# Channel sums as rounded halves times rounded ones, and the keys' partner rows by four small transfers

## The chip, the cores and the metric

The kernel runs on one core of one Trainium2 chip. The metric is the device time of one execution in microseconds, the median of several runs. The core has a matrix engine (TensorE, PE in the rows), a vector engine (VectorE, DVE), a scalar engine (ScalarE, ACT), a general one (GpSimd, POOL) and a queue engine (SyncE, SP). Each engine works through its own list of instructions in the order of that list, and waits on semaphores for the others. Transfers are issued from the lists of SP, ACT and POOL.

## The reference, cut to what matters

Two layers work on 520 tokens (512 of a prompt, 8 of a decode step) with 1024 channels. Each layer takes a root-mean-square norm over the channels, multiplies by one wide input matrix, runs a 31-tap convolution branch and a sliding-window attention branch, and joins the two.

```python
def rms_norm(x, g):
    xf = x.astype(jnp.float32)
    y = xf * lax.rsqrt(jnp.mean(xf * xf, axis=-1, keepdims=True) + EPS)
...
def layer_norm(x, g, b):
    mu = jnp.mean(xf, axis=-1, keepdims=True)
    var = jnp.mean(jnp.square(xf - mu), axis=-1, keepdims=True)
    y = (xf - mu) * lax.rsqrt(var + EPS)
...
    h = rms_norm(x, norm_g)
    z = jnp.einsum('ntd,dc->ntc', h, w_in)
    u = glu[..., :CONV_WIDTH] * jax.nn.sigmoid(glu[..., CONV_WIDTH:])
    c = lax.conv_general_dilated(full, conv_w[:, None, :], ...) + conv_b
    c = jax.nn.silu(layer_norm(c, ln_g, ln_b)) * jax.nn.silu(gate_a)
    y_a = jnp.einsum('ntc,cd->ntd', c, w_conv_out)
    k = partial_rope(k.reshape(n, t, N_KV_HEADS, HEAD_DIM), pos)
    o, new_k, new_v = attend(q, k, v, sinks)
    y_b = jnp.einsum('nte,ed->ntd', o * jax.nn.silu(gate_b), w_attn_out)
    y = jax.nn.sigmoid(mg_a) * y_a + jax.nn.sigmoid(mg_b) * y_b
    return x + jnp.einsum('ntd,de->nte', y, w_out), new_conv, new_k, new_v
```

So three means over the 1024 channels are taken per layer (one of the root-mean-square norm, two of the layer norm), and the final norm takes one more. partial_rope rotates the first 16 of a head's 64 dimensions: dimension d below 8 is paired with d + 8.

## The kernel before

**Layout.** Channels lie on the 128 partitions and tokens along the free axis: a tile `g` is 128 x 520 in fp32, and eight of them hold a 1024-channel activation. All `g` tiles come from one ring of 42 buffers (`gp`, L52 and L69), which the tile framework hands out in program order: a tile can be written only when the tile 42 requests earlier has been read for the last time.

**Products.** A `Unit` (L101 to L145) computes 128 output channels for all tokens. Its weights arrive by SP into `raw` (2 buffers), are rounded on ACT into `whi` (L126, a CAST to fp32r) and subtracted on DVE into the rest `wlo` (L127). `step` (L130) issues three fp32r matmuls of 128x260 for each of eight channel blocks and each half of the tokens: 48 matmuls into one PSUM tile `mm`, of which there are two (L56). A unit can start only when the unit two before it has been copied out of PSUM. The two halves hi and lo of an activation come from `split` (L95), a CAST on ACT and a subtraction on DVE.

**Sums over channels.** `Sum` (L147) adds eight tiles on DVE into `ssum` (L165). `total` (L167) then sums over the partitions with a matmul by a 128x128 matrix of ones, in plain fp32, one for each half of the tokens. `totals` (L175) is called three times per layer: for the first norm (L290), for the layer norm's mean (L609) and for its variance (L615). The final norm calls `total` itself (L695). `rstd` (L178) makes 1/sqrt of a sum: Ln and Exp on ACT (L183, L186) and four operations on DVE (L184 to L189), and `normed` (L268) multiplies the layer's input by it (L271).

**The keys.** After the K unit (L339) its result is copied to `kn` on ACT (L343). A fp32 matmul by a permutation matrix `swap`, once for each half of the tokens (L352), puts each rotated dimension's partner in its row; DVE multiplies that by the sines (L353) and adds (L354). Rows 16 to 63 of a head have a sine of 0.

**The layer norm's place.** Attention scores of 32 blocks run first, interleaved with 16 units for the gates; the convolution (L599, on DVE) fills DVE beside them. Then come the 8 units of the gate GA (L622): each is copied out of PSUM by ACT (L624), gated by a sigmoid (L630) and a product (L631). The sums of the layer norm, the subtraction of the mean (L613) and the squares (L614, by L197) run among these units. Eight units YB (L644), eight YA (L650) and eight of the output product (L675) follow.

**The order.** The order on each engine is set by the tile framework's scheduler, which works from a modelled timeline; `tc.issue_after` and `cur_priority` give it hints. The list of each engine is then fixed. At the start x, the parameters and a table load are issued on ACT (L225, L202, L193), and the first weights and the rest of x on SP.

Of the kernel before, what the change touches and what calls it, by code (L numbers as in the profile page):

```python
# [10 lines left out]
F32R = mybir.dt.float32r  # L11
AF = mybir.ActivationFunctionType
ALU = mybir.AluOpType
# [6 lines left out]
HALF = TOK // 2  # L20
# [3 lines left out]
HD = 64  # L24
# [12 lines left out]
P_G, P_CW, P_CB, P_LG, P_LB, P_SK, P_SS = 0, 8, 256, 264, 272, 280, 296  # L37
N_P = 297

C_ID, C_SW, C_MASK, C_FG = 0, 128, 256, 512  # L40
N_C = 520


@with_exitstack
def hybrid_step(ctx, tc, x_in, w_in, par, const, rope, conv_st, kc_in, vc_in,
                y_out, ncp, nkp, nvp, ncs, nks, nvs):
    nc = tc.nc
    V, A, PE, G = nc.vector, nc.scalar, nc.tensor, nc.gpsimd

    cst = ctx.enter_context(tc.tile_pool(name="cst", bufs=1))  # L50
# [14 lines left out]
    def name(p):  # L65
        uid[0] += 1
        return f"{p}{uid[0]}"

    def g(dt=F32):  # L69
        return gp.tile([128, TOK], dt, tag="g", name=name("g"))  # L70
# [4 lines left out]
    def two(t):  # L75
        return t.rearrange("p (a b) -> p a b", a=2)

    def sbank():
        return psS.tile([128, 512], F32, tag="S", name=name("S"))
# [6 lines left out]

    con = cst.tile([128, N_C], F32, name="con")
    ident = con[:, C_ID:C_ID + 128]
    swap = con[:, C_SW:C_SW + 128]
    ones = cst.tile([128, 128], F32, name="ones")  # L90
    V.memset(ones, 1.0)
    eps = cst.tile([128, 1], F32, name="eps")
    V.memset(eps, EPS)

# [52 lines left out]
    class Sum:  # L147
# [18 lines left out]

        def total(self, hf):  # L167
            ps = sbank()[:, :HALF]
            last = self.left.get(hf)
            PE.matmul(ps, ones, two(self.acc)[:, hf, :], start=True, stop=last is None)  # L170
            if last is not None:
                PE.matmul(ps, ones, last, start=False, stop=True)  # L172
            return ps

        def totals(self):  # L175
            return [self.total(0), self.total(1)]

    def rstd(sums, halves=(0, 1)):  # L178
        y0, v, a = tmp("y0", 1), tmp("v", 1), tmp("a", 1)
# [78 lines left out]
    for l in range(L):  # L258
        last = l + 1 == L
# [19 lines left out]
        for i in range(KT):  # L279
# [39 lines left out]
            if i % 2 == 1:  # L319
# [7 lines left out]
                for i in pair:  # L327
                    V.tensor_tensor(pr4[:, i - i0], st[i0 // 2][:, i - i0],
                                    wv[:, i - i0].unsqueeze(1).broadcast_to([128, NS, TAPS]),
                                    op=ALU.mult)  # L330
# [6 lines left out]


        kps = Unit(l, W_K, hh, hl).both()  # L339
        kn, kcos, ksin, krot = g(), g(), g(), g()  # L340
        nc.gpsimd.dma_start(kcos, rope[2])
        nc.gpsimd.dma_start(ksin, rope[3])
        A.copy(two(kn), kps)  # L343
        V.tensor_tensor(krot, kn, kcos, op=ALU.mult)
        vps = Unit(l, W_V, hh, hl).both()
        vt = g()
        A.copy(two(vt), vps)
        nc.gpsimd.dma_start(nvp[l], vt[:, T - 128:T])
        for hf in range(2):
            c = slice(hf * HALF, (hf + 1) * HALF)  # L350
            kss = sbank()
            PE.matmul(kss[:, :HALF], swap, kn[:, c], start=True, stop=True)  # L352
            V.tensor_tensor(ksin[:, c], kss[:, :HALF], ksin[:, c], op=ALU.mult)  # L353
        V.tensor_tensor(krot, krot, ksin, op=ALU.add)  # L354
        nc.gpsimd.dma_start(nkp[l], krot[:, T - 128:T])
        KH, KL = [], []
        for kv in range(2):
# [9 lines left out]
        for j in range(2):  # L367
            t = g()
# [37 lines left out]
        for j in range(2):  # L406
            t = g()
# [38 lines left out]
        for t in range(8):  # L446
            ps = Unit(l, W_GB + t, hh, hl).both()
# [173 lines left out]
        for i in range(KT):  # L621
            ps = Unit(l, W_GA + i, hh, hl).both()  # L622
# [12 lines left out]
        for i in range(KT):  # L635
            c = cs[i]
# [7 lines left out]
            ps = Unit(l, W_YB + i, oh, ol).both()  # L644
# [4 lines left out]
        for i in range(KT):  # L649
            ps = Unit(l, W_YA + i, ch, cl).both()  # L650
# [17 lines left out]
        if not last:  # L668
# [5 lines left out]
            for i in range(KT):  # L674
                ps = Unit(l, W_OUT + i, yh, yl).both()  # L675
# [68 lines left out]
def _constants():  # L744
    f = np.float32
    con = np.zeros((128, N_C), f)
    r = np.arange(128)
    con[r, C_ID + r] = 1
    d = r % HD
    partner = np.where(d < 8, r + 8, np.where(d < 16, r - 8, r))  # L750
    con[r, C_SW + partner] = 1
    j = np.arange(256)[None, :]
    q = r[:, None]
    ok = np.where(j < 128, j > q, j - 128 <= q)
    con[:, C_MASK:C_MASK + 256] = np.where(ok, 0, NEG)
    pos = np.concatenate([np.arange(T), np.full(NS, PAST)]).astype(f)
    inv = (f(500000.0) ** (-np.arange(0, 16, 2, dtype=f) / f(16))).astype(f)
    ang = pos[None, :] * inv[:, None]
    cos, sin = np.cos(ang).astype(f), np.sin(ang).astype(f)
    rope = np.zeros((4, 128, TOK), f)  # L760
    rope[0] = cos[r % 8]
    rope[1] = sin[r % 8]
    rope[2] = np.where((d < 16)[:, None], cos[d % 8], 1)
    rope[3] = np.where((d < 8)[:, None], -sin[d % 8], np.where((d < 16)[:, None], sin[d % 8], 0))
    return con, rope.astype(f)
# [63 lines left out]
```

## Time and profile before

| what | us |
|---|---|
| median of 3 runs | 1073.75 (1073.62 to 1073.75) |
| the profiled execution | 1073.94 |
| its span in the trace | 1071.8 |
| PE busy | 1058.2 (99%) |
| DVE busy | 855.4 (80%) |
| ACT busy | 515.0 (48%) |
| POOL busy | 77.5 (7%) |

The span is the time from the first to the last instruction of the trace; the profiled execution's own time is 2.1 us longer. PE's matmuls are pipelined: an instruction's own duration (284 ns for a 128x260 one) overlaps the next one's, so what one costs is read from the distance between the starts of two, or from a stretch of the chain that ended last. A plain fp32 matmul shows as two records, an fp32r one as one. Layer 1 repeats layer 0 some 525 us later.

### The profile page before, as it was taken

Reading aid. Unit: us, or ns where it says so; the run is one execution under the profiler, and the core shown is the slowest. Engines: PE = TensorE matmul, PEld = TensorE weight load, DVE = VectorE, ACT = ScalarE, POOL = GpSimd, SP = SyncE. Lnnn points to the kernel's source line nnn. Section 1 sums busy time; section 2 is a strip of 40 time slices with the busy share of each in tenths; the row PEclk is TensorE's granted clock in tenths of the full one; section 3 lists DMA queues with packets and bytes.
Section 4 is the critical chain, followed back from the end, with each engine's and each line's share of the span. In section 5 each row is a group of like instructions: output and inputs, shape, how many; then the busy total and the mean of one; then the engine's idle time right before and its main releaser. Section 6 shows DMA issues by size and latency. Waiting matters only on the chain.

```text
span 1071.8 us, 21521 instructions
## 1 busy us (share of the span) xinstructions
PE 1058.2 (99%) x8738; PEld 1036.0 (97%) x8738; DVE 855.4 (80%) x1570; ACT 515.0 (48%) x951; POOL 77.5 (7%) x185
## 2 busy tenths in 40 slices
PE   8999999999999999999999999999999999999996
PEld 8999999999999999999999999999999999999995
DVE  6999999999999586455569999999999976944545
ACT  7621433366666784223453234334675686822321
POOL 1111211000000000000101113100000000000000
PEclk9999999999999999999999999999999999999998
DMA  7334574332322225233334337623232213242212
GB/s 250 108 119 136 167 245 134 116 100 80 115 79 65 70 69 189 89 99 119 138 92 138 119 126 239 204 100 118 80 119 67 92 41 99 91 171 95 99 59 80
DMA packets 44371, 126.41 MB, mean 118 GB/s; under 512 B 6208, under 2 KB 8976, under 8 KB 44272
## 3 DMA queue, kind: packets, MB, share of 16 engines
q1 hardware_dynamic: 37728, 110.23, 31.0%
q0 software_dynamic: 5104, 13.33, 3.9%
q10 hardware_dynamic: 1440, 1.48, 0.4%
q8 instruction: 68, 1.11, 0.4%
q14 instruction: 31, 0.25, 0.1%
HBM read 107.66 MB, written 17.36 MB: 117 GB/s over the span
## 4 chain that ended last, share of the span: by engine, by line
PE 98%; DVE 1%; DMA 0%; ACT 0%; issue 0%; ACTq 0%; DVEq 0%
PE mm L134 87%; PE S L510 3%; PE pv L545 3%; PE PT L536 2%; PE T L134 1%; DVE g L700 1%; PE V L134 1%; PE S L170 1%; DMA par<-par 0%; PE S L468 0%; PE pvs L490 0%; PE S L352 0%; DVE g L689 0%; PE S L172 0%; PE S L396 0%
## 5 line engine op out<-in xcount | busy, mean ns | idle before, releaser
L134 PE MATMUL mm<-g,whi 128*128 128x260 f32 x4160 | 772.8, 284 | 1.9 <-ACT g L212 1.8
L134 PEld LDWEIGHTS mm<-g,whi 128*128 128x128 f32 x4160 | 647.6, 189 | 8.5 <-issue 5.7
L134 PE MATMUL mm<-g,wlo 128*128 128x260 f32 x2080 | 589.1, 283 | 0.0
L134 PEld LDWEIGHTS mm<-g,wlo 128*128 128x128 f32 x2080 | 392.4, 189 | 0.9 <-issue 0.8
L599 DVE SCALAR_TENSOR_TENSOR acc<-u,par,acc 128x512 f32<-128x512 f32 x464 | 328.3, 743 | 0.2
L126 ACT CAST whi<-raw 128x1024 fp32r<-128x1024 f32 (+2 forms) x166 | 172.6, 1040 | 207.7 <-PE mm L134 167.8
L127 DVE TENSOR_TENSOR wlo<-raw,whi 128x1024 fp32r<-128x1024 f32 (+2 forms) x166 | 200.3, 1208 | 53.5 <-ACT whi L126 53.3
L134 PE MATMUL mm<-o,whi 128*128 128x260 f32 x992 | 179.3, 282 | 1.0 <-DVE g L689 1.0
L134 PEld LDWEIGHTS mm<-o,whi 128*128 128x128 f32 x992 | 153.1, 188 | 1.5 <-issue 0.8
L134 PE MATMUL mm<-o,wlo 128*128 128x260 f32 x496 | 139.5, 282 | 0.0
L134 PEld LDWEIGHTS mm<-o,wlo 128*128 128x128 f32 x496 | 93.2, 188 | 0.0
L522 ACT ACTIVATE p<-p,sm 128x257 f32<-128x257 f32 (+1 forms) x128 | 60.8, 478 | 10.7 <-DVE sm L516 10.6
L538 ACT COPY pts<-PT 128x256 f32<-128x256 f32 (+1 forms) x64 | 33.8, 528 | 60.6 <-PE PT L536 60.3
L516 DVE CUSTOM_DVE_ANT_0 p<-S,con,nsk 128x256 f32<-128x256 f32 (+1 forms) x128 | 52.6, 446 | 10.8 <-PE PT L536 8.9
L514 POOL COPY p<-nsk 128x2 f32<-128x2 f32 x64 | 21.7, 345 | 351.5 <-PE PT L536 276.4
L651 DVE TENSOR_TENSOR g<-mm,g 128x520 f32<-128x520 f32 x16 | 11.2, 699 | 42.9 <-PE mm L134 42.9
L510 PE MATMUL S<-g,g 128*128 128x256 f32 x256 | 42.4, 285 | 0.0
L449 ACT ACTIVATE g<-mm 128x520 f32<-128x520 f32 x16 | 9.7, 605 | 56.8 <-PE mm L134 56.8
L645 DVE TENSOR_TENSOR g<-mm,g 128x520 f32<-128x520 f32 x16 | 11.1, 695 | 32.1 <-PE mm L134 32.1
L510 PEld LDWEIGHTS S<-g,g 128*128 128x128 f32 x256 | 35.2, 188 | 0.8 <-DVE sm L516 0.8
L536 PE MATMUL PT<-con,p 128*128 128x128 f32 x224 | 35.6, 276 | 0.0
L526 ACT ACTIVATE p<-p,sm 128x128 f32<-128x128 f32 (+1 forms) x64 | 29.9, 480 | 8.9 <-DVE sm L525 8.9
(169 smaller groups left out, 821.0 us busy)
## 6 DMA issues: line engine op xcount, KB each, us to landing
raw<-w SPq DMA_DIRECT2D x162, 512.0 KB, 3.4
qscr<-g SPq DMA_DIRECT2D x32, 256.0 KB, 4.4
g<-qscr SPq DMA_DIRECT2D x32, 256.0 KB, 3.7
g<-x SPq DMA_DIRECT2D x15, 260.0 KB, 4.8
g<-rope POOLq DMA_DIRECT2D x8, 260.0 KB, 4.6
xres<-g POOLq DMA_DIRECT2D x8, 260.0 KB, 2.3
g<-xres SPq DMA_DIRECT2D x8, 260.0 KB, 5.1
g<-conv_state POOLq DMA_DIRECT2D x8, 248.0 KB, 3.2
```

Of the source, the lines that this page charges most:

```text
L126: mark[2] = A.copy(self.hi[:, ks, :], self.raw[:, ks, :])
L127: mark[0] = V.tensor_tensor(self.lo[:, ks, :], self.raw[:, ks, :], self.hi[:, ks, :].bitcast(F32), op=ALU.subtract)
L134: mark[1] = PE.matmul(self.acc[hf], a[:, k, :], b[k][:, c], start=(k == 0 and j == 0), stop=(k == KT - 1 and j == 2))
L510: PE.matmul(S3[:, kv, :], qs[t, kv][:, b * 128:b * 128 + 128], K[kv][:, k0:k0 + 256], start=(j == 0), stop=(j == 1))
L514: G.tensor_copy(p[:, :, nk:nk + 1], nsk[:, 2 * t:2 * t + 2].unsqueeze(2))
L516: V.tensor_tensor_reduce(out=p[:, kv, :nk], in0=S3[:, kv, :nk], in1=con[:, C_MASK + 256 - nk:C_MASK + 256], op0=ALU.add, op1=ALU.min, scal ...
L522: exp_ins[0] = A.activation(p[:, kv, :nk + 1], p[:, kv, :nk + 1], AF.Exp, bias=nm[:, kv:kv + 1], scale=-1.0, accum_out=dn[:, kv:kv + 1])
L526: A.mul(p[:, 0, :nk], p[:, 0, :nk], dn[:, 0:1])
L536: PE.transpose(PT[:, kv, kb, :], p[:, kv, kb * 128:kb * 128 + 128], ident)
L538: A.copy(pts[t][:, :, j0:j0 + nb, :], PT[:, :, :nb, :])
L545: PE.matmul(pv[kv * 64:kv * 64 + 64, j * 128:(j + nb) * 128], vb[:, j * 128 + kv * 64:j * 128 + kv * 64 + 64], pts[t][:, kv, 2 * j:2 * j + ...
L599: V.scalar_tensor_tensor(dst, us[i][:, k:k + T], cw(i, k), acc[i], op0=ALU.mult, op1=ALU.add)
```

## The change

`totals` no longer multiplies the fp32 sum by fp32 ones. It splits the sum with `split` (a CAST on ACT into a `g` tile, a subtraction on DVE into another), and multiplies both by `ones_r`, the ones rounded to fp32r: two fp32r matmuls per half in place of one fp32 matmul. `ones_r` is made by ACT at the start of the program. The final norm's `total` stays fp32. For the keys, a tile `ks` is set to zero by POOL, four transfers of 8 rows each on POOL's queue copy the partner rows out of `kn`, and DVE multiplies the whole tile by the sines once. The permutation matrix leaves the constants.

```diff
--- before.py
+++ after.py
@@ -37,8 +37,8 @@
 P_G, P_CW, P_CB, P_LG, P_LB, P_SK, P_SS = 0, 8, 256, 264, 272, 280, 296
 N_P = 297
 
-C_ID, C_SW, C_MASK, C_FG = 0, 128, 256, 512
-N_C = 520
+C_ID, C_MASK, C_FG = 0, 128, 384
+N_C = 392
 
 
 @with_exitstack
@@ -86,9 +86,10 @@
 
     con = cst.tile([128, N_C], F32, name="con")
     ident = con[:, C_ID:C_ID + 128]
-    swap = con[:, C_SW:C_SW + 128]
     ones = cst.tile([128, 128], F32, name="ones")
     V.memset(ones, 1.0)
+    ones_r = cst.tile([128, 128], F32R, name="onesr")
+    A.copy(ones_r, ones)
     eps = cst.tile([128, 1], F32, name="eps")
     V.memset(eps, EPS)
 
@@ -166,14 +167,17 @@
 
         def total(self, hf):
             ps = sbank()[:, :HALF]
-            last = self.left.get(hf)
-            PE.matmul(ps, ones, two(self.acc)[:, hf, :], start=True, stop=last is None)
-            if last is not None:
-                PE.matmul(ps, ones, last, start=False, stop=True)
+            last = self.left[hf]
+            PE.matmul(ps, ones, two(self.acc)[:, hf, :], start=True, stop=False)
+            PE.matmul(ps, ones, last, start=False, stop=True)
             return ps
 
         def totals(self):
-            return [self.total(0), self.total(1)]
+            parts, sums = split(self.acc), [sbank()[:, :HALF] for _ in range(2)]
+            for hf, ps in enumerate(sums):
+                for j, t in enumerate(parts):
+                    PE.matmul(ps, ones_r, two(t)[:, hf, :], start=(j == 0), stop=(j == 1))
+            return sums
 
     def rstd(sums, halves=(0, 1)):
         y0, v, a = tmp("y0", 1), tmp("v", 1), tmp("a", 1)
@@ -337,21 +341,21 @@
 
 
         kps = Unit(l, W_K, hh, hl).both()
-        kn, kcos, ksin, krot = g(), g(), g(), g()
+        kn, ks, kcos, ksin, krot = g(), g(), g(), g(), g()
+        G.memset(ks, 0.0)
         nc.gpsimd.dma_start(kcos, rope[2])
         nc.gpsimd.dma_start(ksin, rope[3])
         A.copy(two(kn), kps)
+        for r in (0, HD):
+            for d in (0, 8):
+                nc.gpsimd.dma_start(ks[r + d:r + d + 8, :], kn[r + 8 - d:r + 16 - d, :])
         V.tensor_tensor(krot, kn, kcos, op=ALU.mult)
         vps = Unit(l, W_V, hh, hl).both()
         vt = g()
         A.copy(two(vt), vps)
         nc.gpsimd.dma_start(nvp[l], vt[:, T - 128:T])
-        for hf in range(2):
-            c = slice(hf * HALF, (hf + 1) * HALF)
-            kss = sbank()
-            PE.matmul(kss[:, :HALF], swap, kn[:, c], start=True, stop=True)
-            V.tensor_tensor(ksin[:, c], kss[:, :HALF], ksin[:, c], op=ALU.mult)
-        V.tensor_tensor(krot, krot, ksin, op=ALU.add)
+        V.tensor_tensor(ks, ks, ksin, op=ALU.mult)
+        V.tensor_tensor(krot, krot, ks, op=ALU.add)
         nc.gpsimd.dma_start(nkp[l], krot[:, T - 128:T])
         KH, KL = [], []
         for kv in range(2):
@@ -747,8 +751,6 @@
     r = np.arange(128)
     con[r, C_ID + r] = 1
     d = r % HD
-    partner = np.where(d < 8, r + 8, np.where(d < 16, r - 8, r))
-    con[r, C_SW + partner] = 1
     j = np.arange(256)[None, :]
     q = r[:, None]
     ok = np.where(j < 128, j > q, j - 128 <= q)
```

The change asks the ring for two more `g` tiles per sum and for one more per layer, and the scheduler sets another order. Three places follow; the names are the program's (a number behind an underscore tells tiles apart, and differs between the two kernels for the same tile).

ACT in the layer norm of layer 0, before: `mm_4551` and `mm_4613` are the first two GA units, `S_4484` and `S_4486` the mean's sums, `whi_4732` weights of a later unit.

```order
L526 ACTIVATE p_4126<-p_4126,sm_4128 128x256
L624 COPY g_4600<-mm_4551 128x520
L97 CAST o_4176<-sq_4172 128x520
L126 CAST whi_4732<-raw_4731 128x1024
L628 ACTIVATE g_3943<-g_3943 128x520
L627 ACTIVATE g_4060<-g_4060 128x520
L628 ACTIVATE g_4161<-g_4161 128x520
L610 ACTIVATE a_4483<-S_4484 128x260
L610 ACTIVATE a_4483<-S_4486 128x260
L624 COPY g_4662<-mm_4613 128x520
```

The same stretch after: `mm_4572` and `mm_4634` are the first two GA units, `u_0` to `u_7` the convolution's results, `ssum_4508` the variance's sum on DVE and `g_4537` its rounded half.

```order
L201 ACTIVATE sq_4510<-u_1_405 128x520
L98 CAST o_4224<-sq_4220 128x520
L201 ACTIVATE sq_4514<-u_2_555 128x520
L201 ACTIVATE sq_4518<-u_3_689 128x520
L201 ACTIVATE sq_4522<-u_4_816 128x520
L201 ACTIVATE sq_4526<-u_5_933 128x520
L201 ACTIVATE sq_4530<-u_6_1060 128x520
L201 ACTIVATE sq_4534<-u_7_1177 128x520
L98 CAST g_4537<-ssum_4508 128x520
L628 COPY g_4621<-mm_4572 128x520
L628 COPY g_4683<-mm_4634 128x520
L634 ACTIVATE sq_4625<-g_4621 128x520
```

The copies of the first two GA units (L624 before, L628 now) stood one ahead of and one right behind the mean (L610); now both stand behind the squares and the rounding of the variance's sum.

PE at the end of the second GA unit in layer 0, before: the mean's sums by `ones`, the unit's last nine products, a block of attention transposes and the third GA unit `mm_4675`.

```order
L134 MATMUL mm_4613<-g_467,whi_4608 128x260
L170 MATMUL S_4484<-ssum_4475,ones 128x260
L170 MATMUL S_4486<-ssum_4475,ones 128x260
L134 MATMUL mm_4613<-g_472,whi_4608 128x260
L134 MATMUL mm_4613<-g_472,wlo_4609 128x260
L134 MATMUL mm_4613<-g_473,whi_4608 128x260
...
L134 MATMUL mm_4613<-g_616,wlo_4609 128x260
L134 MATMUL mm_4613<-g_617,whi_4608 128x260
L536 MATMUL PT_4184<-con,p_4025 128x128 x4
L134 MATMUL mm_4675<-g_319,whi_4670 128x260
L134 MATMUL mm_4675<-g_319,wlo_4671 128x260
```

After: the unit's end, transposes `PT`, the mean's sums in four products, the attention values `pv`, the first product of the variance's sums, and the third GA unit `mm_4696`.

```order
L135 MATMUL mm_4634<-g_625,whi_4629 128x260
L540 MATMUL PT_4193<-con,p_4034 128x128 x4
L179 MATMUL S_4497<-g_4493,onesr 128x260
L179 MATMUL S_4498<-g_4493,onesr 128x260
L179 MATMUL S_4497<-g_4494,onesr 128x260
L179 MATMUL S_4498<-g_4494,onesr 128x260
L540 MATMUL PT_4199<-con,p_4082 128x128 x4
L549 MATMUL pv_4211<-pts_3975,g_1469 64x256 x2
L540 MATMUL PT_4205<-con,p_4135 128x128 x4
L549 MATMUL pv_4211<-pts_3975,g_1469 64x256 x4
L549 MATMUL pv_4211<-pts_3975,g_1469 64x128 x2
L179 MATMUL S_4541<-g_4537,onesr 128x260
```

Before, the variance's sums stood some 230 rows behind the mean's; now they stand right behind the last attention values and ahead of the third GA unit, which begins two rows below the last one shown.

ACT at the first norm of layer 0, before: casts of weights (`whi_403`, `whi_493`, `whi_553`), copies out of PSUM, and Ln and Exp (`y_300`) of the sums.

```order
L302 COPY g_313<-mm_103 128x260 x2
L126 CAST whi_403<-raw_402 128x1024
L306 COPY u_0_311<-mm_107 128x520
L126 CAST whi_493<-raw_492 128x1024
L183 ACTIVATE y_300<-S_296,eps 128x260
L183 ACTIVATE y_300<-S_298,eps 128x260
L186 ACTIVATE y_300<-y_300 128x520
L126 CAST whi_553<-raw_552 128x1024
```

After: `g_298` is the rounded half of the sum `ssum_175`.

```order
L127 CAST whi_411<-raw_410 128x1024
L310 COPY u_0_319<-mm_109 128x520
L127 CAST whi_501<-raw_500 128x1024
L98 CAST g_298<-ssum_175 128x520
L306 COPY g_321<-mm_105 128x260 x2
L127 CAST whi_561<-raw_560 128x1024
L187 ACTIVATE y_308<-S_302,eps 128x260
L187 ACTIVATE y_308<-S_303,eps 128x260
L190 ACTIVATE y_308<-y_308 128x520
```

The cast of the third weights (`whi_553` before, `whi_561` now) moved ahead of Ln, and the sum's own cast came in behind the second one. On DVE the rest of that weight (`wlo`) moved in the same way ahead of the sum's first use (L188, L184 before).

At the start of ACT's list the load of `ones_r`'s copy routine and the copy itself now stand ahead of the transfer of the parameters.

## Rows read from the trace of the kernel before

**Rows 1.** The page: busy time per engine, and the chain that ended last.

```profile
PE 1058.2 (99%) x8738; PEld 1036.0 (97%) x8738; DVE 855.4 (80%) x1570; ACT 515.0 (48%) x951; POOL 77.5 (7%) x185
PE 98%; DVE 1%; DMA 0%; ACT 0%; issue 0%; ACTq 0%; DVEq 0%
```

**Rows 2.** Waits of PE: who waited, for whom, us in total, times, longest.

```profile
PE mm L134 <- ACT g L212: 1.8, 1, 1.8
```

**Rows 3.** PE's groups by form: shapes, count | busy us, mean ns | idle before.

```profile
L170 PE MATMUL S<-ssum,ones 128*128 128x260 f32 x28 | 7.5, 386 | 1.2 <-DVE ssum L165 1.2
L352 PE MATMUL S<-g,con 128*128 128x260 f32 x8 | 2.1, 382 | 0.0
```

**Rows 4.** Chain that ended last, 340 to 400 us: start, us, what, records.

```profile
354.73 0.88 PE S L170 x4
355.61 1.08 PE mm L134 x9
356.69 0.44 PE PT L536 x4
...
372.48 1.23 PE pv L545 x12
```

**Rows 5.** The same chain, 100 to 125 us, around the keys' permutation.

```profile
113.06 0.88 PE S L352 x4
...
120.24 4.80 PE mm L134 x40
```

**Rows 6.** ACT in time, 20 to 32 us: start, us, what, [idle before, releaser].

```profile
22.00 1.08 ACT L126 CAST whi<-raw 128x1024 fp32r<-128x1024 f32 x1
24.22 0.92 ACT L183 ACTIVATE y<-S,eps 128x260 f32<-128x260 f32 x2 [1.14 <-PE S L170]
...
26.57 1.05 ACT L126 CAST whi<-raw 128x1024 fp32r<-128x1024 f32 x1 [0.76 <-PE V L134]
```

**Rows 7.** DVE in time, 20 to 32 us.

```profile
19.57 2.31 DVE L165 TENSOR_TENSOR ssum<-ssum,sq 128x520 f32<-128x520 f32 x3
...
27.93 1.22 DVE L127 TENSOR_TENSOR wlo<-raw,whi 128x1024 fp32r<-128x1024 f32 x1
29.06 2.10 DVE L271 SCALAR_TENSOR_TENSOR sq<-g,par,v 128x520 f32<-128x520 f32 x3
```

**Rows 8.** Busy us of PE, PEld, DVE, ACT, POOL (count) in 40 to 50 us.

```profile
40.00:50.00 10.00, 10.00 (x84) 9.82 (x83) 10.00 (x18) 4.79 (x8) 2.70 (x5) 1.00 0.39 133
```

**Rows 9.** PE in time around 49 us.

```profile
48.94 0.28 PE L134 MATMUL mm<-g,wlo 128*128 128x260 f32 x1
49.20 0.51 PE L134 MATMUL mm<-g,whi 128*128 128x260 f32 x2
```

**Rows 10.** ACT in time, 354 to 363 us.

```profile
355.85 0.57 ACT L624 COPY g<-mm 128x520 f32<-128x520 f32 x1
356.32 0.63 ACT L97 CAST o<-sq 128x520 fp32r<-128x520 f32 x1
...
359.39 0.64 ACT L610 ACTIVATE a<-S 128x260 f32<-128x260 f32 x2
```

**Rows 11.** DVE in time, 358 to 375 us.

```profile
360.06 4.97 DVE L613 TENSOR_TENSOR u<-u,a 128x520 f32<-128x520 f32 x8 [0.91 <-ACT a L610]
```

**Rows 12.** The same columns near the start, then granted clock, DMA share, GB/s.

```profile
8.00:10.00 2.00, 2.00 (x11) 2.00 (x11) 0.59 (x1) 1.46 (x2) 0.00 (x0) 0.50 1.04 408
10.00:12.00 2.00, 2.00 (x14) 2.00 (x13) 1.99 (x4) 1.82 (x4) 0.00 (x0) 0.65 1.04 404
```

**Rows 13.** ACT's head: the parameters' issue and the table load.

```profile
1.19 0.45 ACTq L202 DMA_DIRECT2D par<-par  x1
1.67 1.28 ACT L193 ACT_TABLE_LOAD   x1 [1.67 <-PEq L801]
```

**Rows 14.** POOL's transfers, 103 to 125 us: count, KB each, median us to landing.

```profile
g<-vc POOLq DMA_DIRECT2D x2, 256.0 KB, 6.0
...
ncp<-u POOLq DMA_DIRECT2D x1, 15.0 KB, 1.7
```

## The prediction

> **What bounds the kernel now.** I read the page's busy shares and chain first. PE is busy 99% of the span and 98% of the chain that ended last is PE [rows 1], so the time is PE's work plus PE's holes. Then I read PE's waits: the longest is 1.8 us at the start, for the first rounded activations [rows 2]. So two things count: the PE time that the change takes away, and any hole that it opens. Then I read the chain piece by piece for prices, since a matmul's own duration overlaps the next one's. Last I laid the new order of ACT, DVE and PE beside the times of before, to find who would be late.
>
> **PE work taken away.** One fp32 sum is two records; `L170` has 28, that is 14 matmuls [rows 3], of which 12 are in `totals` and change (two are the final norm's). On the chain a pair of them costs 0.88 us, so 0.44 each [rows 4]. The new products have the shape of a unit's products, and nine of those take 1.08 us, 0.12 each [rows 4]. 12 x 0.44 = 5.3 go and 24 x 0.12 = 2.9 come: -2.4 us. The permutation is 8 records, 4 matmuls over both layers [rows 3], and a pair costs 0.88 [rows 5]: -1.75 us. Together -4.1 us, all on the path, since PE is the path. The price of 0.12 is that of fp32r products of this shape; no row shows one by ones, but nothing in the shape differs.
>
> **The layer norm: a hole in each layer.** This term decides. Before, the first GA unit's copy out of PSUM came at 355.85 and the second's right behind the mean [rows 10]; two PSUM tiles serve all units, so PE went on. In the new order both copies stand behind the rounding of the variance's sum (`g_4537`), and on PE the first product of that sum stands ahead of the third GA unit. Either alone holds PE until the whole chain from mean to variance is done. I walk that chain on the clock of before:
>
> - PE ends the second GA unit at 356.69 - 0.88 = 355.8, the mean's sums no longer being inside it [rows 4].
> - ACT reaches the mean later: the first copy (0.47 to the next start) becomes the sum's cast (about the same), and a further weight cast (1.05, as in [rows 6]) and a copy of transposes (0.5, as [rows 10] show for a copy) now stand ahead. The mean started at 359.39 and ends 0.64 later [rows 10]; now it ends near 361.6. A weight remainder on DVE (1.22, [rows 7]) ends there too.
> - DVE subtracts the mean from eight tiles: 4.97 [rows 11], to 366.6. Then three short operations of the attention output, estimated at 1.0: 367.6.
> - ACT casts that output between the second and the third square, so six squares wait for it. DVE adds seven squares and takes one remainder, 8 x 0.62 (4.97 / 8): 372.5. The squares (0.53 apart, as the casts and copies in [rows 10]) stay just ahead.
> - The sum's cast, 0.63 as the cast in [rows 10]: 373.1. The first copy, 0.57: 373.7. Only then can the third GA unit start.
>
> Meanwhile PE has only four split products (0.48), three blocks of transposes (3 x 0.44, [rows 4]), eight value products (1.23 x 8/6 = 1.6, [rows 4]) and two split ones (0.24): 3.7 us. The hole is 373.7 - 355.8 - 3.7 = 14.2 us. Layer 1 has the same order in all three places, so 28.4 us in all. From below: if the attention output (1.0) and its remainder (0.6) fall outside the chain, 12.6 a layer. From above: if one more weight cast and remainder (1.05 + 1.22) come in front, 16.5. Behind the hole I see no second one: PE has then two units free to run, and the variance's own result is wanted only by the YA units, some 14 units later.
>
> **The clock behind the hole.** After the one wait of 1.8 us [rows 2], the granted clock was 0.50 in 8 to 10 us and 0.65 in 10 to 12 [rows 12], that is, mostly the lower of the two levels (1.2 of 2.4 GHz), and 1 before and after. That cost 2 x 0.5 + 2 x 0.35 = 1.7 us. I take the same after each hole: 3.4 us. Below: nothing (no loss is seen behind smaller waits); above: twice that, since the hole is longer and broken by short work.
>
> **The first norm of layer 0.** The order puts the third weight cast ahead of Ln on ACT, and its remainder ahead of the sum's use on DVE. That cast starts at 26.57, when PE leaves the unit whose buffer it takes [rows 6]; PE is 0.4 earlier (two fp32 sums less four products), so 26.2, and it ends at 27.2. Ln started at 24.22 [rows 6] and the first use of the norm (L271) at 29.06 [rows 7], with a remainder between them on DVE: 4.84 less about 1.13 is 3.7 from Ln. Now Ln starts at 27.2, and the remainder stands ahead of `v`, which delays it by another 0.4: L271 at 31.3, later by 2.25. From there DVE is full up to the last remainder that PE wants (10.00 of 10 us in 40 to 50, [rows 8]), and PE already waits for it: a product starts at 48.94 and the next, which should come 0.12 later, at 49.20 [rows 9], so 0.14 of waiting. With DVE full, the delay comes through whole: PE arrives 0.4 earlier and waits till 49.2 + 2.25, that is 2.8, or +2.65 net. One weight remainder more or less (1.22) gives 1.4 to 3.9. In layer 1 the sum is ready long before PE gets to it, and I take nothing.
>
> **The head.** The parameters' transfer was issued at 1.19, ahead of a table load of 1.28 [rows 13], and PE's first wait ends by it. It now stands behind another table load and a cast. An issue needs only the queue's own part of ACT, not its compute part, so I take 0.1; if the issue has to wait until the cast is done, 1.28 + 0.25 = 1.5.
>
> **The keys.** The copy of `kn` ends near 108 and PE wants the result at 120.24 (the products beyond the transposes [rows 5]) at the earliest. POOL issues four transfers at some half a microsecond each, so the last leaves near 110; a small one landed in 1.7 us and the slowest of that stretch in 6.0 [rows 14]: 111.8 to 116. DVE's product then waits up to 2.6 us, with a cover of about 4 on the weight remainders behind it. I take nothing. If that cover is gone, what is over it is paid in PE time. The Trainium skill ("SBUF — State Buffer", section "SBUF: two separate sides") says that transfers issued by GpSimd wait for their descriptors while VectorE runs an operation that holds the shared port, with 620 ns growing to about 3100. The rows speak against it here: the transfer of 1.7 us [rows 14] ran beside a DVE that was all but full.
>
> **The sum.** On the profiled execution (1073.94): -2.4 - 1.75 + 28.4 + 3.4 + 2.65 + 0.1 = +30.4, so 1104.3. The median of before is 0.19 lower, so 1104.2 us.
>
> **The rivals.**
> - *PE is not held (faster or equal).* If PE's list were not kept strictly, or the copies ran ahead of the cast, both holes vanish: -4.1 + 2.65 + 0.1 = 1072.4 us, within the bound of no change; without the first norm's wait 1069.7. It decides at a hole of 0.7 us per layer, where the sum is zero. Against it: PE stood idle at 49.06 with other products queued behind the waiting one [rows 9], and the tiles' ring puts the copy's target behind the split's. 3% each.
> - *A shorter hole.* If parts of the chain overlap that I put end to end (squares ahead of the attention output, a mean as early as before), 8 to 12 us a layer: 1090 to 1099. 13%.
> - *The clock stays low longer*, so that it costs 5 us or more per hole instead of 1.7: 1111 and more. For it: the hole is eight times the one seen. 10%.
> - *Late small transfers.* With the 1.7 us of the small one grown by a factor of five (8.5), the last lands near 118.6, DVE waits 5 us and PE some 1.4 per layer: 1107. That is the mechanism of the page named above. 4%.
> - *The products by ones are no cheaper than fp32* (0.44 instead of 0.12): 24 x 0.32 = +7.7, 1112. 3%.
>
> **How the numbers follow.** The forecast (hole between 12.6 and 16.5 us per layer, clock up to 3.4) has 64%. Its own ends: -4.1 + 25.2 + 0 + 1.4 = 1096.3, and up, with not all terms at their upper ends at once, 1112. The range takes in the late transfers and the dearer products: 1096 to 1113; the shorter hole's lower part, the longer clock's upper part and the kernel that isn't held stay out, some 2 in 10. A measurement of this kernel can tell about 0.2% (2.1 us) from no change. Faster by that: 3%. Within it: 3%. Slower: 94%.
>
> **What would show it.** In the changed kernel's waits of PE, a new line for the sums (L179) with two waits of some 9 to 14 us, or the same split over L540 and L549, released by ACT's casts and copies; PE idle near 356 to 374 and 525 us later; a lower granted clock behind each. Near 49 us a wait of 2 to 3 us for DVE. No wait of PE near 120. If PE's waits sum to under 10 us, the walk through the layer norm is wrong; if the hole is there but longer, a link of it (the attention output's cast between the squares) is longer than I took; if the K stretch waits, the transfers are.

## The result and the profile after

The changed kernel takes 1105.34 us (median of 5 runs, 1104.65 to 1106.5) against 1073.75 before: a ratio of 1.0293, 95% interval 1.028 to 1.0306. It is 31.6 us slower, where 30.4 were forecast. The profiled execution took 1105.12 us, its span is 1103.3 (1071.8 before).

The page of the changed kernel gives the busy shares and the chain, the lines that answer to [rows 1]:

```profile
PE 1063.6 (96%) x8730; PEld 1037.9 (94%) x8730; DVE 859.7 (78%) x1574; ACT 519.9 (47%) x959; POOL 83.1 (8%) x195
PE 92%; DVE 4%; ACT 3%; issue 1%; DMA 0%; DVEq 0%; ACTq 0%
```

PE is no longer the whole chain: 7% of it runs over DVE and ACT, most of that around the two layer norms, where PE first still works and then waits. The waits of PE (who for whom, us in total, times, longest) name the places. Before, none was longer than the one at the start [rows 2]:

```profile
PE S L179 <- ACT g L98: 18.3, 3, 7.5
PE PT L540 <- ACT pts L542: 4.0, 2, 3.8
PE mm L135 <- ACT g L216: 1.7, 1, 1.7
PE pv L549 <- ACT pts L542: 1.4, 2, 0.7
...
PE mm L135 <- DVE g L99: 1.1, 2, 0.6
PE mm L135 <- ACT g L98: 1.1, 1, 1.1
```

L179 are the products of the split sums, L98 the cast that makes their rounded half. The 18.3 us are the layer norm's two variance sums (7.5 each) and the mean's sum in layer 1 (3.3). The 4.0 and 1.4 us are the attention's transposes and values in the same holes. The last two lines are the first norm near 49 us. The third line, 1.7 us, is the wait at the start that was there before.

PE in layer 0, in time: the instructions with the long waits, and the first product of the third GA unit (start, us, what, [idle before, releaser]):

```profile
361.86 1.11 PE L540 MATMUL PT<-con,p 128*128 128x128 f32 x4 [3.76 <-ACT pts L542]
...
365.75 2.40 PE L549 MATMUL pv<-pts,g 128*64 128x256 f32 x12 [0.68 <-ACT pts L542]
375.63 0.58 PE L179 MATMUL S<-g,onesr 128*128 128x260 f32 x1 [7.48 <-ACT g L98]
...
376.22 0.48 PE L135 MATMUL mm<-g,whi 128*128 128x260 f32 x1
```

The same stretch on ACT, with the mean, the attention output's cast, the variance sum's cast and the two late copies, which before stood at 355.85 and right behind the mean [rows 10]:

```profile
361.70 0.66 ACT L614 ACTIVATE a<-S 128x260 f32<-128x260 f32 x2
...
368.92 0.62 ACT L98 CAST o<-sq 128x520 fp32r<-128x520 f32 x1 [2.16 <-DVE sq L554]
...
374.95 0.62 ACT L98 CAST g<-ssum 128x520 fp32r<-128x520 f32 x1 [1.78 <-DVE ssum L166]
375.48 1.08 ACT L628 COPY g<-mm 128x520 f32<-128x520 f32 x2
```

And on DVE, the subtractions [rows 11] and what follows them:

```profile
362.50 4.96 DVE L617 TENSOR_TENSOR u<-u,a 128x520 f32<-128x520 f32 x8
368.19 0.69 DVE L554 TENSOR_TENSOR sq<-pv,g 128x512 f32<-128x512 f32 x1 [0.73 <-PE pv L549]
...
370.19 4.72 DVE L166 TENSOR_TENSOR ssum<-ssum,sq 128x520 f32<-128x520 f32 x6
```

This is the chain that the prediction walked, in its order, but for one piece: from 361.86 to 368.19 us it ran over PE's transposes and values (L540, L549) and not over the subtractions, which were done at 367.46, so that DVE waited 0.73 us for PE. The granted clock (last but two of the columns; PE's busy us come first) went down inside the hole and came back only behind it:

```profile
358.00:362.00 4.00, 0.24 (x2) 0.14 (x2) 2.01 (x3) 4.00 (x9) 0.00 (x0) 0.71 0.36 102
...
370.00:374.00 4.00, 0.00 (x0) 0.00 (x0) 3.58 (x6) 3.00 (x6) 0.00 (x0) 0.50 0.00 0
374.00:378.00 4.00, 2.37 (x10) 2.38 (x11) 2.38 (x5) 3.03 (x6) 0.00 (x0) 0.50 0.00 0
378.00:382.00 4.00, 4.00 (x28) 4.00 (x27) 1.24 (x3) 2.39 (x4) 0.00 (x0) 0.73 0.00 0
```

Where the time went can be read from the starts of the same instructions in both traces:

| first instruction of | before, us | after, us | later by |
|---|---|---|---|
| attention scores, layer 0 (L510, now L514) | 206.5 | 206.9 | 0.4 |
| YB gating, layer 0 (L645, now L649) | 402.3 | 419.7 | 17.4 |
| norm of layer 1 (L271, now L275) | 551.1 | 568.1 | 17.0 |
| attention scores, layer 1 | 731.2 | 746.7 | 15.5 |
| YB gating, layer 1 | 927.3 | 959.0 | 31.7 |
| end of the span | 1071.8 | 1103.3 | 31.5 |

The stretch with the layer norm loses 17.0 us in layer 0 and 16.2 in layer 1; everything else together gains 1.7.

### The profile page after: what moved, and what is told of

The parts are those of the page before. It is cut to its first block, busy times and chain, and to the rows that moved or that the text cites. A ratio compares the mean times of both kernels' runs of the same rounds, so it can differ in the third digit from the quotient of the medians.

```text
span 1103.3 us, 21547 instructions
## 1 busy us (share of the span) xinstructions
PE 1063.6 (96%) x8730; PEld 1037.9 (94%) x8730; DVE 859.7 (78%) x1574; ACT 519.9 (47%) x959; POOL 83.1 (8%) x195
## 4 chain that ended last, share of the span: by engine, by line
PE 92%; DVE 4%; ACT 3%; issue 1%; DMA 0%; DVEq 0%; ACTq 0%
PE mm L135 82%; PE S L514 3%; PE pv L549 3%; PE PT L540 2%; PE T L135 1%; ACT g L631 1%; DVE ssum L166 1%; ACT g L632 1%; DVE g L704 1%; PE V L135 1%; PE S L179 0%; DVE acc L603 0%; DMA par<-par 0%; PE S L472 0%; PE pvs L494 0%
## 5 line engine op out<-in xcount | busy, mean ns | idle before, releaser
L514 PE MATMUL S<-g,g 128*128 128x256 f32 x256 | 42.4, 285 | 0.0
L540 PE MATMUL PT<-con,p 128*128 128x128 f32 x224 | 37.8, 288 | 4.1 <-ACT pts L542 4.0
L649 DVE TENSOR_TENSOR g<-mm,g 128x520 f32<-128x520 f32 x16 | 11.1, 696 | 33.6 <-PE mm L135 33.6
L549 PE MATMUL pv<-pts,g 128*64 128x256 f32 (+1 forms) x256 | 35.0, 394 | 1.4 <-ACT pts L542 1.4
L514 PEld LDWEIGHTS S<-g,g 128*128 128x128 f32 x256 | 35.1, 189 | 0.4 <-DVE sm L520 0.4
```

Source lines behind the costliest of these rows:

```text
L514: PE.matmul(S3[:, kv, :], qs[t, kv][:, b * 128:b * 128 + 128], K[kv][:, k0:k0 + 256], start=(j == 0), stop=(j == 1))
L540: PE.transpose(PT[:, kv, kb, :], p[:, kv, kb * 128:kb * 128 + 128], ident)
L549: PE.matmul(pv[kv * 64:kv * 64 + 64, j * 128:(j + nb) * 128], vb[:, j * 128 + kv * 64:j * 128 + kv * 64 + 64], pts[t][:, kv, 2 * j:2 * j + ...
```

## The experiments

The theory: the copies of the first two GA units out of PSUM are held behind the variance's cast, because both take tiles of the ring of 42 and the ring is handed out in program order; PE, which also has the variance's products ahead of the third GA unit, stands until the whole layer norm chain is done. The first rival: the longer way from a sum to its product (cast, subtraction, four products) holds PE wherever the tiles are. The other questions are what the clock, the first norm and the keys cost by themselves. The verdict on each run is by its median against the kernel before on the same chip (1073.8 to 1074.0).

### Split halves outside the ring

```diff
-            parts, sums = split(self.acc), [sbank()[:, :HALF] for _ in range(2)]
+            kinds = iter(("y0", "v"))
+            parts = split(self.acc, new=lambda dt: ap.tile([128, TOK], dt,
+                          tag=(k := next(kinds)), bufs=1, name=name(k)))
+            sums = [sbank()[:, :HALF] for _ in range(2)]
```

> The changed kernel with one edit: the two halves of a split sum go into the buffers of y0 and v (which rstd uses right after) and no longer into tiles of the ring of 42. The ring theory: the copies of the GA units stand ahead of the variance's cast again, both holes of some 15 to 17 us go, what stays is -4.1 us of PE work, about +2 at the first norm and up to 1 a layer for PE waiting on the mean's halves: 1071 to 1074 us. The rival, that the longer way from sum to product (cast, subtraction) holds PE whatever buffers it uses: above 1090 us, with PE waiting for the cast of the variance's sum.

Measured: 1074.01 us, ratio 1.0 (0.9991 to 1.0009). PE's waits in the layer norm are gone; these short ones are the largest that the trace has left there:

```profile
PE S L181 <- DVE v L99: 0.2, 1, 0.2
PE PT L542 <- ACT pts L544: 0.2, 1, 0.2
PE mm L135 <- ACT g L630: 0.2, 1, 0.2
```

Every cast, subtraction and product of the change is still there, so the latency of the split by itself is not what holds PE, neither for the variance nor for the mean. 31 us hang on which buffers two tiles come from.

### The ring tiles named earlier, the copies written where they were

```diff
+        ready_s = [g() for _ in range(2)]
         R2 = rstd(sm.totals())
 ...
-            s = g()
+            s = ready_s.pop(0) if ready_s else g()
```

> The changed kernel with one edit: the two ring tiles that the first two GA units are copied into are named ahead of the variance's total in the program text, so that they come ahead of the split's tiles in the ring by name. The copies are still written behind the total. If the ring hands a tile out at its naming, the holes go: 1071 to 1074 us. If it hands it out at the first instruction that writes it, in program order, the copies stay behind the cast and the holes stay: 1103 to 1107 us.

Measured: 1105.72 us, ratio 1.0295 (1.0276 to 1.0313), with the same line among PE's waits as in the changed kernel:

```profile
PE S L179 <- ACT g L98: 18.3, 3, 7.5
```

On ACT the variance's cast still comes first, and the copies, into the two tiles named earlier (L629), behind it:

```profile
376.06 0.62 ACT L98 CAST g<-ssum 128x520 fp32r<-128x520 f32 x1 [1.77 <-DVE ssum L166]
376.60 1.08 ACT L629 COPY g<-mm 128x520 f32<-128x520 f32 x2
```

Naming a tile earlier does nothing. That the place of its first write in the program text is what counts is the next run's to show.

### The first four GA units written ahead of the variance's total

```diff
+        gated(0, 4)
         R2 = rstd(sm.totals())
         for c in cs:
             V.tensor_tensor(c, c, R2, op=ALU.mult)
+        gated(4, KT)
```

(`gated(lo, hi)` is the loop over the GA units, L622 to L631.)

> The changed kernel with one edit: the first four GA units with their copies are written ahead of the variance's total in the program text; all split halves stay in the ring. If the holes come from the ring being handed out in the program order of the first writes, the copies go ahead and the holes with them: 1073 to 1076 us, as with buffers outside the ring. If the ring's size or the split's latency holds PE, above 1085 us.

Measured: 1084.37 us, ratio 1.0099 (1.0084 to 1.0115). The two waits of 7.5 us are gone, as the theory has it, with all split halves still in the ring, so it isn't their number in the ring that held PE. But 10 us of loss are left, which I had not expected. The waits show why:

```profile
PE mm L135 <- ACT g L625: 3.8, 1, 3.8
PE S L179 <- ACT g L98: 3.3, 1, 3.3
```

In layer 0 the two copies stand ahead of the mean (L614) now, but behind the mean's cast, four gate sigmoids and a weight cast on ACT (the copies run from 361.20 to 362.27), so PE waits 3.8 us for the first of them. In layer 1 it is the mean's cast that is late by 3.3. So there is a second, smaller hole around the mean; the next run tells more of it. That the scheduler hands the ring out in the order of first writes is concluded from this run and the two before it; no trace shows the scheduler's own working. The changed kernel has waits of the same size in the same place (the 3.76 of layer 0, for a copy of transposes, and the 3.3 of layer 1), ahead of the large one.

### Only the mean's total split

```diff
-                R = rstd(sq.totals())
+                R = rstd(sq.totals(True))
 ...
-        R2 = rstd(sm.totals())
+        R2 = rstd(sm.totals(True))
```

(`totals(True)` is the plain fp32 sum of before.)

> The changed kernel with the first norm's and the variance's totals in plain fp32 as before; only the mean's is split (keys by transfers as in the change). The ring theory: two ring tiles whose data is early hold nobody; PE work falls by 1.75 + 2 x 0.4 = 2.55 us, PE waits up to 1 us a layer for the mean's halves: 1071 to 1073.5 us. The rival, that a split sum among the GA units costs a hole by its own latency: 1080 us or more.

Measured: 1084.17 us, ratio 1.0094 (1.0081 to 1.0108). The ring theory's size was wrong. The rival's number (1080 or more) came, but not its reason, as the rows below show. PE's waits have no variance any more, and the mean's cast twice:

```profile
PE S L186 <- ACT g L98: 6.6, 2, 3.3
```

ACT in layer 0 of this run, the mean's cast and the copies of the first two GA units:

```profile
357.48 0.61 ACT L98 CAST g<-ssum 128x520 fp32r<-128x520 f32 x1
...
359.42 1.08 ACT L635 COPY g<-mm 128x520 f32<-128x520 f32 x2
```

And in the run with the halves of mean and variance in y0 and v and no such wait (the first norm's total plain, further down), the first copy and the mean's cast:

```profile
355.11 0.57 ACT L637 COPY g<-mm 128x520 f32<-128x520 f32 x1
...
358.65 0.62 ACT L98 CAST y<-ssum 128x520 fp32r<-128x520 f32 x1
```

There the cast comes still later, and holds nobody, because a copy has gone ahead of it and PE has the third GA unit to run. With the halves in the ring both copies stand behind the mean's cast, as they do behind the variance's in the changed kernel. So the second hole is of the same kind as the large one; it is smaller because the mean's cast ends at 358.1 us, and the variance's in the changed kernel at 375.6. What failed in the expectation is that the mean's data would be early enough to hold nobody.

The clock in layer 0, in 2 us each, says why 3.3 us of waiting cost more than twice that:

```profile
354.00:356.00 2.00, 0.82 (x6) 0.42 (x4) 0.50 (x1) 2.00 (x5) 0.00 (x0) 1.00 0.04 8
356.00:358.00 2.00, 0.00 (x0) 0.00 (x0) 1.34 (x2) 2.00 (x5) 0.00 (x0) 1.00 0.14 23
358.00:360.00 2.00, 1.62 (x6) 1.22 (x7) 1.62 (x2) 2.00 (x5) 0.00 (x0) 0.64 0.67 240
360.00:362.00 2.00, 2.00 (x9) 0.91 (x8) 1.22 (x3) 1.53 (x5) 0.00 (x0) 0.50 0.34 78
362.00:364.00 2.00, 2.00 (x10) 2.00 (x10) 2.00 (x4) 0.00 (x0) 0.00 (x0) 0.50 0.47 184
364.00:366.00 2.00, 2.00 (x14) 2.00 (x13) 2.00 (x4) 0.00 (x0) 0.00 (x0) 0.66 0.00 0
```

The clock was still 1.00 while PE stood and fell after PE had begun again; some 2 x (0.36 + 0.5 + 0.5 + 0.34) = 3.4 us are lost with PE almost fully at work. From the first scores to the first YB this stretch takes 202.2 us against 195.8 before: 6.4 more, for a wait of 3.3.

### Only the variance's total split

```diff
-                R = rstd(sq.totals())
+                R = rstd(sq.totals(True))
 ...
-        for hf, s in enumerate(sm.totals()):
+        for hf, s in enumerate(sm.totals(True)):
```

> The changed kernel with the first norm's and the mean's totals in plain fp32 as before; only the variance's is split (keys by transfers). The ring theory: this alone makes nearly the whole loss, two holes of 14 to 17 us: 1073.75 - 2.55 + 28 to 34 = 1099 to 1105 us. The rival, that the holes need both splits of the layer norm: below 1090 us.

Measured: 1103.6 us, ratio 1.0279 (1.0263 to 1.0295), with the changed kernel's waits in full:

```profile
PE S L186 <- ACT g L98: 15.0, 2, 7.5
PE PT L547 <- ACT pts L549: 8.2, 2, 4.1
```

The variance's two tiles alone make nearly all of the loss, as the theory has it.

### Filling the hole with unused matmuls: what the clock costs

```diff
+        fill = psT.tile([128, 512], F32, tag="T", name=name("fill"))
+        for _ in range(16):
+            PE.matmul(fill[:, :128], ones, ones, start=True, stop=True)
         R2 = rstd(sm.totals())
```

> The changed kernel with 16 fp32 matmuls of 128x128 ones (results unused) behind the last attention values and ahead of the variance's products, in both layers; they fit in the hole. If the lower clock behind and in the hole costs some 2 to 5 us a layer, PE runs at the full clock again when the third GA unit starts, and the time falls by 2 to 8 us: 1097 to 1103 us. If the clock costs nothing beyond the wait, it stays at 1105 us or rises.

Measured: 1104.28 us, ratio 1.0283 (1.0269 to 1.0297), 1.1 us under the changed kernel's 1105.34, less than expected and not clear of the scatter (1103.9 to 1105.11 here, 1104.65 to 1106.5 there). The 16 ran at the lower clock first and at the full one from about 370.6 us on, and were done 2.9 us too early; the clock fell again behind that gap. So I lengthened them to 29:

```diff
-        for _ in range(16):
+        for _ in range(29):
```

> The changed kernel with 29 unused fp32 matmuls of 128x128 in the hole of each layer in place of 16. Sixteen ran from 368.8 to 373.4 us and left a gap of 2.9 us, behind which the granted clock fell again (0.50 in 378 to 380) with the units already running. With 29 the gap should be about half a microsecond. If the clock behind the hole is what is paid (1.9 us a layer by the granted clock of 374 to 382 us in the changed kernel), the time falls by 3 to 4 us against the 1105.3 of the changed kernel: 1101 to 1103 us. If it costs nothing, 1104 to 1106.

Measured: 1102.71 us, ratio 1.0266 (1.0251 to 1.0282). The fill ran from 369.41 for 7.9 us and the units behind it had the full clock:

```profile
374.00:376.00 2.00, 2.00 (x20) 2.00 (x19) 1.79 (x3) 0.51 (x1) 0.00 (x0) 1.00 0.00 0
376.00:378.00 2.00, 2.00 (x18) 1.88 (x17) 0.95 (x2) 1.72 (x4) 0.00 (x0) 1.00 0.00 0
378.00:380.00 2.00, 2.00 (x19) 2.00 (x18) 1.31 (x2) 1.98 (x3) 0.00 (x0) 1.00 0.00 0
```

From the first scores to the first YB it takes 211.0 and 210.3 us in the two layers against 212.8 and 212.3 in the changed kernel: 1.8 and 2.0 us are what the lower clock behind the hole costs. (The medians differ by 2.6; this run's first norm was over a microsecond later.)

### The first norm: put back, and split alone

The variant with the halves in y0 and v, the first norm's total plain again:

```diff
-                R = rstd(sq.totals())
+                R = rstd(sq.totals(True))
```

> The variant with the split halves in the buffers of y0 and v, and with the first norm's total in plain fp32 as before. If the first norm's late chain is the other part of what the change cost, PE's three waits near 49 us (2.2 us) go back to 0.14, and the time is 1073.75 - 1.75 (keys) - 4 x 0.4 (split mean and variance) = 1070.4 us, up to 1071.5 if PE waits for the mean's halves. If the first norm costs nothing on the whole, it stays at the 1074.0 of that variant.

Measured: 1070.26 us, ratio 0.9967 (0.9954 to 0.9979). The waits near 49 us are gone, and 3.75 us with them, two more than the 1.8 (2.56 less 0.8 of PE work) that I made out for the first norm. Some 0.6 of these two belong to the attention values of layer 0, as the run with the keys alone shows below.

The other way round, the keys by transfers and the first norm's total alone split (mean and variance plain):

```diff
-        for hf, s in enumerate(sm.totals()):
+        for hf, s in enumerate(sm.totals(True)):
 ...
-        R2 = rstd(sm.totals())
+        R2 = rstd(sm.totals(True))
```

> The kernel with keys by transfers and only the first norm's total split, mean and variance in plain fp32 (against 1070.85 us with the keys alone). If the late chain of layer 0 costs what the prediction has it (2.65 us net of a wait of 0.14), less 0.8 us of PE work in two layers: 1072.7 us, 1071.5 to 1073.9. If the first norm's wait was made by the later edits of the order, 1070 us.

Measured: 1071.33 us, ratio 0.9977 (0.9968 to 0.9987), just under what was expected, and only 0.5 above the run with the keys alone. The three waits are there (1.1, 0.57, 0.56 us), and the copy of the keys is 2.8 us later (110.0 against 107.2). By the second layer's keys 1.7 of these are left, and by its YA units 0.8. So one pair of runs puts the net price of the split first norm at 3.75 us and the other at 0.5, with intervals of 2 us and more on each ratio: its place is shown, its price isn't settled.

### The keys alone, and the sums alone

The kernel before with the keys' transfers and no split sum (the change's edits at the keys alone):

```diff
-            PE.matmul(kss[:, :HALF], swap, kn[:, c], start=True, stop=True)
-            V.tensor_tensor(ksin[:, c], kss[:, :HALF], ksin[:, c], op=ALU.mult)
 ...
+                nc.gpsimd.dma_start(ks[r + d:r + d + 8, :], kn[r + 8 - d:r + 16 - d, :])
 ...
+        V.tensor_tensor(ks, ks, ksin, op=ALU.mult)
```

> The kernel before with the keys' partner rows by transfers alone, all totals in plain fp32. If the transfers are hidden (as the trace of the changed kernel has it, no wait of PE near 120 us), four matmuls of 0.44 go: 1072.0 us. If the four transfers or their waits on DVE are paid elsewhere, 1073.5 or more.

Measured: 1070.85 us, ratio 0.9973 (0.9961 to 0.9984): 2.9 us faster, with an interval of 1.7 to 4.2. The transfers show no wait of PE. From the first scores to the last one this kernel takes 133.5 us and the one before 134.1 (133.8 and 134.4 in layer 1), in both cases with PE at work throughout, so a part of the gain lies in a stretch that the edit doesn't touch except by its order. The chains show it. Before, one group of four records of attention values (two fp32 products) in each layer is broken by a block of scores:

```profile
289.01 0.58 PE pv L545 x2
289.59 0.67 PE S L510 x4
290.26 0.58 PE pv L545 x2
```

With the keys alone that group is whole, as the other groups of four are:

```profile
288.46 0.58 PE pv L555 x4
```

Two records cost as much as four, so the break costs 0.58 us a layer. Four matmuls of 0.44 and two breaks make the 2.9.

The changed kernel with the permutation product put back (the same lines the other way round, the totals all split):

```diff
-                nc.gpsimd.dma_start(ks[r + d:r + d + 8, :], kn[r + 8 - d:r + 16 - d, :])
 ...
+            PE.matmul(kss[:, :HALF], swap, kn[:, c], start=True, stop=True)
```

> The changed kernel with the keys' partner rows by the permutation product as before, all three totals split. If the keys have no part in the holes, the loss is that of the changed kernel plus what the keys' transfers save (1.75 by the chain's prices, 2.9 by the run with the keys alone): 1107 to 1108.5 us. If the transfers make part of the loss, below 1105 us.

Measured: 1107.09 us, ratio 1.0308 (1.0292 to 1.0323), 1.75 above the changed kernel. The holes are there without the transfers (PE waits 17.7 us for the casts of the sums and 6.1 for the copies of transposes, against 18.3 and 4.0 in the changed kernel), so the keys don't make them. That the difference is just the price of the permutation is in part chance: these waits alone differ by 1.5.

### A version that keeps the gain

The halves in y0 and v, the keys by transfers, and the first norm plain in layer 0 alone:

```diff
-                R = rstd(sq.totals())
+                R = rstd(sq.totals(l == 0))
```

> The variant that split mean and variance in the buffers of y0 and v, with the first norm's total plain in layer 0 only and split in layer 1, where the sum is ready some 8 us before PE takes it. If layer 1's split is hidden, the 0.4 us of PE work comes off the 1070.26 of that variant: 1069.9 us, between 1069.2 and 1070.6. If layer 1's first norm pays the same wait as layer 0's, 1072 us or more.

Measured: 1069.86 us, ratio 0.9963 (0.9949 to 0.9976). It beats the kernel before by 0.4% and the changed one by 3.2%. Against the run with the keys alone (1070.85) the split sums bring some 1 us by the medians, less than the intervals of the two ratios can tell apart, where five split totals of 0.4 us less PE work each would make 2.0; most of the gain is the keys'.

## Why the prediction was right, step by step

- **The hole in the layer norm: right in place and mechanism, too small by 1.5 a layer.** Forecast 14.2 us and 1.7 of clock per layer, that is 15.9; measured 17.0 and 16.2, and with the 0.8 us of PE work saved in the same stretch 17.8 and 17.0. The runs showed the cause that was forecast: outside the ring no hole, the variance's tiles alone nearly the whole. Three links were undersized; in layer 0 the third GA unit starts at 376.22, forecast 373.7. The seven additions were taken at 0.62 us, the pitch of eight independent subtractions [rows 11]; additions into one sum depend on each other and took 4.72 / 6 = 0.79 each, so that they and the remainder took 6.1 us and not 5.0. [rows 7] had that number (2.31 for three is 0.77) and I took it from the wrong row. The mean ended at 362.4, forecast 361.6. And the short PE work inside the hole ran at the lower clock (12 records of values in 2.40 us, where [rows 4] have 1.23), so DVE waited 0.73 us for it, and the attention output took 1.3 us and not 1.0.
- **The second, smaller hole** inside the large one was not named: the mean's ring tiles hold the same copies, behind a cast that itself stands behind ACT's sigmoids. It costs next to nothing extra while the large hole is there (1103.6 us with only the variance split, where the first norm's waits are missing too, against 1105.3), and 6 us a layer when it isn't. The walk had the mean's lateness but not that this alone would hold PE.
- **The clock: right for what stands behind the hole.** 1.7 us forecast per hole; 1.8 and 2.0 by filling it. The clock fell inside the hole already (0.93 in 358 to 360, 0.50 in 360 to 362), which the forecast left out and which made the work in there slow. The rival of a clock that stays low much longer fell: it was back 4 us after PE resumed.
- **The first norm: right in size where it happens.** L271's successor starts at 31.27, forecast 31.3; PE's three waits cost 1.26 + 0.72 + 0.72 = 2.7 us with the 0.12 of normal pitch taken off each, against 0.14 before: 2.56 net, forecast 2.65.

```profile
31.27 2.10 DVE L275 SCALAR_TENSOR_TENSOR sq<-g,par,v 128x520 f32<-128x520 f32 x3
```

```profile
48.65 0.39 PE L135 MATMUL mm<-g,whi 128*128 128x260 f32 x1 [1.11 <-ACT g L98]
...
49.96 0.51 PE L135 MATMUL mm<-g,whi 128*128 128x260 f32 x2 [0.57 <-DVE g L99]
...
51.51 0.51 PE L135 MATMUL mm<-g,whi 128*128 128x260 f32 x2 [0.55 <-DVE g L99]
```

- **The head: right that the issue doesn't wait for the copy.** The parameters' transfer went out at 1.25, inside the table load that stands ahead of it, and the first product's input was 0.06 us earlier than before:

```profile
1.19 1.28 ACT L92 ACT_TABLE_LOAD   x1 [1.19 <-PEq L803]
1.25 0.39 ACTq L206 DMA_DIRECT2D par<-par  x1
...
5.35 0.73 ACT L216 ACTIVATE g<-g,par 128x520 fp32r<-128x520 f32 x1 [0.59 <-DMA par<-par]
```

- **The keys: hidden, as forecast.** The four small transfers landed in 1.8 us beside a DVE that was busy throughout (1.00 of each us from 108 to 114), near the lower bound of 1.7 [rows 14], and PE has no wait there. The rule of the Trainium skill that the rival of late transfers drew on ("SBUF — State Buffer", section "SBUF: two separate sides": transfers issued by GpSimd wait for their descriptors beside certain VectorE operations) shows nowhere here.

```profile
g<-g POOLq DMA_DIRECT2D x4, 16.2 KB, 1.8
```

- **The PE work: right in price, not closed in sum.** The split products ran as priced (two in 0.24 us at the full clock). But the terms as measured (34.8 for the two layer norms, 2.56, -0.06, -4.1) make 33.2, and the span grew by 31.5. Of the missing 1.7 us of gain some 0.6 are the attention values of layer 1, whose broken group is whole in the changed kernel (that of layer 0 is still broken). The rest lies in stretches where only the order differs, and no run here took it apart. So the total came out closer than its terms: a hole 3 us too small and a gain 1.7 us too small partly cancel.
- **The other rivals.** PE was not let past the waiting product. The products by ones cost no more than others. A shorter hole did not come.

## What to carry to other kernels

Before a tile of a shared ring is added, look at what else is first written to that ring behind it in the program text: with a scheduler that hands the ring out in that order, a tile that is late in data can hold the first writes behind it, an evacuation of PSUM among them, as it did here. Give such late, short-lived tiles a buffer of their own, or one that the next step overwrites anyway. And price a chain of operations that each need the one before from a row of just such a chain, not from independent ones.

## What the runs showed of the hardware that I had not expected

- A hole of PE can cost twice its length. With only the mean split, a wait of 3.3 us made a stretch 6.4 us longer; the granted clock stayed 1.00 during the wait, and was 0.64, 0.50, 0.50 and 0.66 in the four stretches of 2 us from 358 on. So about half of the loss stood behind the wait. In the changed kernel the clock fell while PE still waited (0.50 in 360 to 362, the wait of 3.76 ended at 361.86).
- Filling the hole only partly does little: behind 16 matmuls that ended 2.9 us early the clock was low at 378 to 380 us again, and the median fell by 1.1 us, within the scatter; 29 gave back 1.8 and 2.0 us in the two layers.
- Additions into the same tile follow each other at 0.77 to 0.79 us, independent ones of the same shape at 0.62.
- A group of four records of attention values took 0.58 us on PE and a group of two as much, so one block of scores between them cost 0.58 us a layer, with PE busy all the while.
